# State space matrices and rotation tables made in another layer's stage and kept in DRAM

## The chip, the cores and the metric

The kernel runs on one core of a Trainium2 chip. The metric is the time of one execution on the device in microseconds; the time given is the median of three runs. The core has a matrix engine (TensorE, PE in the profile), a vector engine (VectorE, DVE), an activation engine (ScalarE, ACT), a general engine (GpSimd, POOL) and a queue that issues most of the DMAs (SyncE, SP). Each engine works through its own instructions in the order in which the program holds them.

## What is computed

A first block of two layers and a second block of one layer run over 1024 positions (and 16 learned ones in the first block) of width 1024, in float32. Each layer of the first block mixes the positions in three ways, gates and joins the results (`mix`) and adds an output product:

```python
for l in range(DEPTH):                       # 2
    u = rms_norm(h, norm_w[l]) @ w_in[l]
    ...                                      # three mixers, each times silu of a gate
    h = h + mix @ w_out[l]
```

The second block has four branches of width 256; the change is about the first, a diagonal state space with 16 groups of 64 complex states, whose matrices depend on the weights alone:

```python
mag = jnp.exp(lam_re * dt); ang = lam_im * dt
lb_re = mag * jnp.cos(ang); lb_im = mag * jnp.sin(ang)
den = jnp.square(lam_re) + jnp.square(lam_im); nr = lb_re - 1.0
f_re = (nr * lam_re + lb_im * lam_im) / den
f_im = (lb_im * lam_re - nr * lam_im) / den
bb_re = f_re[..., None] * b_re - f_im[..., None] * b_im
bb_im = f_re[..., None] * b_im + f_im[..., None] * b_re
bu_re, bu_im = ...                           # inputs times bb
_, _, x_re, x_im = lax.associative_scan(combine, (a_re, a_im, bu_re, bu_im), axis=1)
y = einsum(x_re, c_re) - einsum(x_im, c_im) + d * ug
y = jax.nn.gelu(y.reshape(bsz, s, BRANCH_WIDTH))
y = y * jax.nn.sigmoid(y @ glu_w + glu_b)
```

The other branches are two attentions and a recurrent mixer; then come gates (32 products of 1024 by 1024 positions, `sigmoid(gates)`), a merge, and a feed-forward part.

## The kernel before, in words

Activations lie with 128 channels on the partitions and positions along the free axis, so a matrix of width 1024 is eight tiles. A float32 product is three passes: values and weights are split into a high and a low part (`hh`, `hl`; `wih`, `wil`), and high by high, low by high and high by low are added in one PSUM bank (L159 to L161). ACT makes the high part of a weight, GpSimd the low one (L153). Tiles come from shared pools: 29 slots, 11 temporaries (`temp`), 6 weight tiles, 2 side tiles; a tile that is asked for waits until the oldest of its pool is free.

*The output products of a layer* (`first_half`): for each of eight row tiles f, `proj` (L163) multiplies the eight tiles of `mx` by the weight `wo`, in three chunks of 348 positions. VectorE adds the residual to each chunk (`hn`, L788), and once all three are done the tile goes to DRAM (`spill`) and is normed in part (`hh` on ACT, `hl` and the sum of squares `sq` on VectorE). `proj` takes a function `along`, which it calls in the middle and at the end of each chunk; here nothing is given.

*The state space's stage* (class `S5`). The positions are cut by four: four neighbours are stacked on the partitions, so 256 steps remain for the scan. `into` shuffles the products of the first weight, 32 channels at a time, into `su`, in turn on ACT and VectorE. `small` works out the powers of the transition from 8-column tiles (62 tiny instructions of VectorE). `matrices` multiplies these into the input matrices `b` (VectorE) and the output matrices `d` (GpSimd), `turned` transposes `b` on TensorE (`s5t`) into `e`, `tables` builds two pairs of rotation tables of 256 steps by doubling (`s5cos`, `s5sin`; the first on VectorE, the second on GpSimd), and `within` makes the matrix `k` of what a step does to itself and its three neighbours (`s5k`). Then `run` walks four blocks of states through `two`, a generator of five steps: input products `bu` on TensorE; a rotation by the tables, with two of its adds on GpSimd (`sw`); four scans on VectorE; the rotation back (`sx`), one of its adds on GpSimd; the output products `sy`. Two blocks are under way at a time, one step behind each other. `gate` applies gelu and the sigmoid gate.

*The gate products* are a filler: `c.feed(us)` puts gate matmuls (`fg`, with weights `fw` split by ACT and VectorE) worth so many microseconds into TensorE's program where it is called, from one list of 512 triples of products that starts in the recurrent stage and whose remainder is worked off after the attentions. In the state space's stage it is called between the steps of `two`.

The order of each engine's instructions is the scheduler's: it follows the order in which the code asks for them, but puts an instruction ahead where its inputs are there early.

Of the kernel before, what the change touches and what calls it, by code (L numbers as in the profile page):

```python
# [12 lines left out]
F32 = mybir.dt.float32  # L13
# [643 lines left out]
def first_half(c, a, vec):  # L657
# [4 lines left out]
    for l in range(2):  # L662
# [799 lines left out]
class S5:  # L1462
# [8 lines left out]
    T = 4  # L1471
    N = 256

    def __init__(self, c, a, project, consts, dcol):
        self.c, self.a, self.dcol = c, a, dcol
        self.u = [c.slot("su") for _ in range(2)]
        self.k = c.slot("s5k")
        c.nc.gpsimd.memset(self.k[:, :1024], 0.0)
        self.small()
        project(0, self.into(self.u[0]))  # L1480
        self.matrices()
        project(1, self.into(self.u[1]))
        self.turned()
        self.tables()
        c.feed(4)
        self.within()
# [18 lines left out]
    def small(self):  # L1505

        c, nc, a = self.c, self.c.nc, self.a
        v = nc.vector
        TT = v.tensor_tensor
        par = c.cp.tile([P, 24], F32, name="s5par", tag="s5par", bufs=1)  # L1510
        nc.sync.dma_start(out=par, in_=a["s5_par"])
        self.bc = bc = c.temp("s5bc")
        nc.sync.dma_start(out=bc[:, :1024], in_=a["s5_bc"])
        lre, lim, ldt = (par[:, 8 * i : 8 * i + 8] for i in range(3))
        sm = c.cp.tile([P, 176], F32, name="s5sm", tag="s5sm", bufs=1)
        w = iter(sm[:, 8 * i : 8 * i + 8] for i in range(22))
        dt, mag, ang, k, si, co = (next(w) for _ in range(6))
        nc.scalar.activation(dt, ldt, AF.Exp)
        TT(mag, lre, dt, ALU.mult)
        nc.scalar.activation(mag, mag, AF.Exp)  # L1520
        TT(ang, lim, dt, ALU.mult)

        v.tensor_scalar(k, ang, 1.0 / (2 * math.pi), 12582912.0, ALU.mult, ALU.add)
        v.tensor_scalar(k, k, -12582912.0, None, ALU.add)
        for part in TURN:
            v.scalar_tensor_tensor(ang, k, -part, ang, ALU.mult, ALU.add)
        v.tensor_scalar(ang, ang, PI_BELOW, -PI_BELOW, ALU.min, ALU.max)
        nc.scalar.activation(si, ang, AF.Sin)
        nc.scalar.activation(co, ang, AF.Sin, scale=0.5)
        TT(co, co, co, ALU.mult)  # L1530
        v.tensor_scalar(co, co, -2.0, 1.0, ALU.mult, ALU.add)
        nr, li, den, t1, fre, fim = (next(w) for _ in range(6))
        TT(nr, mag, co, ALU.mult)
        TT(li, mag, si, ALU.mult)

        pw = c.cp.tile([P, 4 * 32], F32, name="s5pw", tag="s5pw", bufs=1)
        x = [pw[:, 32 * i : 32 * i + 32].rearrange("p (j l) -> p j l", j=8) for i in range(4)]
        self.up, self.down = x[:2], x[2:]
        (ur, ui), (dr, di) = self.up, self.down
        v.tensor_copy(ur[:, :, 0], nr)  # L1540
        v.tensor_copy(ui[:, :, 0], li)
        for l in range(1, 4):
            TT(ur[:, :, l], ur[:, :, l - 1], nr, ALU.mult)
            TT(t1, ui[:, :, l - 1], li, ALU.mult)
            TT(ur[:, :, l], ur[:, :, l], t1, ALU.subtract)
            TT(ui[:, :, l], ur[:, :, l - 1], li, ALU.mult)
            TT(t1, ui[:, :, l - 1], nr, ALU.mult)
            TT(ui[:, :, l], ui[:, :, l], t1, ALU.add)
        v.memset(dr[:, :, 3], 1.0)
        v.memset(di[:, :, 3], 0.0)  # L1550
        for o, i in ((dr, ur), (di, ui)):
            for s in range(3):
                v.tensor_copy(o[:, :, s], i[:, :, 2 - s])

        self.m4, self.c4, self.s4 = (next(w) for _ in range(3))
        TT(self.m4, mag, mag, ALU.mult)
        TT(self.m4, self.m4, self.m4, ALU.mult)
        c2, s2 = (next(w) for _ in range(2))
        for ci, si_, co_, so_ in ((co, si, c2, s2), (c2, s2, self.c4, self.s4)):
            TT(co_, si_, si_, ALU.mult)  # L1560
            v.tensor_scalar(co_, co_, -2.0, 1.0, ALU.mult, ALU.add)
            v.scalar_tensor_tensor(so_, si_, 2.0, ci, ALU.mult, ALU.mult)

        v.tensor_scalar(nr, nr, -1.0, None, ALU.add)
        TT(den, lre, lre, ALU.mult)
        TT(t1, lim, lim, ALU.mult)
        TT(den, den, t1, ALU.add)
        v.reciprocal(den, den)
        TT(fre, nr, lre, ALU.mult)
        TT(t1, li, lim, ALU.mult)  # L1570
        TT(fre, fre, t1, ALU.add)
        TT(fre, fre, den, ALU.mult)
        TT(fim, li, lre, ALU.mult)
        TT(t1, nr, lim, ALU.mult)
        TT(fim, fim, t1, ALU.subtract)
        TT(fim, fim, den, ALU.mult)
        self.fre, self.fim = fre, fim

        self.dq = c.cp.tile([P, 8], F32, name="s5dq", tag="s5dq", bufs=1)
        d2 = self.dq.rearrange("p (t j) -> p t j", t=2)  # L1580
        for s in range(4):
            for j in range(4):
                nc.scalar.copy(d2[32 * s : 32 * s + 32, :, j], self.dcol[32 * j : 32 * j + 32, :])

    def matrices(self):

        c, nc = self.c, self.c.nc
        v, g = nc.vector, nc.gpsimd
        bc = self.bc
        q = lambda x: x.rearrange("p (j h) -> p j h", j=8)  # L1590
        bre, bim, cre, cim = (q(bc[:, 256 * i : 256 * i + 256]) for i in range(4))
        f = lambda x: x.unsqueeze(2).to_broadcast([P, 8, 32])
        bb = c.temp("s5bb")
        o = [q(bb[:, 256 * i : 256 * i + 256]) for i in range(4)]
        TT = v.tensor_tensor
        TT(o[0], bre, f(self.fre), ALU.mult)
        TT(o[2], bim, f(self.fim), ALU.mult)
        TT(o[0], o[0], o[2], ALU.subtract)
        TT(o[1], bim, f(self.fre), ALU.mult)
        TT(o[3], bre, f(self.fim), ALU.mult)  # L1600
        TT(o[1], o[1], o[3], ALU.add)
        every = lambda x: x.unsqueeze(2).to_broadcast([P, 8, 4, 32])
        power = lambda x: x.unsqueeze(3).to_broadcast([P, 8, 4, 32])
        r4 = lambda x: x[:, :1024].rearrange("p (j l h) -> p j l h", j=8, l=4)

        def product(e, re, im, xr, xi, p, sign):

            t = c.temp("s5t")
            e.tensor_tensor(r4(re), every(xr), power(p[0]), ALU.mult)
            e.tensor_tensor(r4(t), every(xi), power(p[1]), ALU.mult)  # L1610
            e.tensor_tensor(re[:, :1024], re[:, :1024], t[:, :1024], ALU.subtract)
            t = c.temp("s5t")
            e.tensor_tensor(r4(im), every(xr), power(p[1]), ALU.mult)
            e.tensor_tensor(r4(t), every(xi), power(p[0]), ALU.mult)
            if sign > 0:
                e.tensor_tensor(im[:, :1024], im[:, :1024], t[:, :1024], ALU.add)
            else:
                v.scalar_tensor_tensor(im[:, :1024], im[:, :1024], -1.0, t[:, :1024], ALU.mult, ALU.subtract)

        self.b = [c.temp("s5b") for _ in range(2)]  # L1620
        product(v, *self.b, o[0], o[1], self.down, 1)
        self.d = [c.slot("s5d") for _ in range(2)]
        product(g, *self.d, cre, cim, self.up, -1)

        self.d0 = c.cp.tile([P, 512], F32, name="s5d0", tag="s5d0", bufs=1)
        nc.scalar.copy(self.d0[:, 0:256], bc[:, 512:768])
        nc.scalar.activation(self.d0[:, 256:512], bc[:, 768:1024], AF.Copy, scale=-1.0)

    def turned(self):

        c, nc = self.c, self.c.nc
        self.e = [c.slot("s5e") for _ in range(2)]
        for r in range(2):
            for h in range(2):
                ps = c.bank("s5t")
                for j in range(4):
                    o = slice((4 * h + j) * P, (4 * h + j + 1) * P)
                    nc.tensor.transpose(ps[:, j * P : (j + 1) * P], self.b[r][:, o], c.ident)
# [768 lines left out]
```

## Time and profile before

| | us |
|---|---|
| median of three runs (3210.05 to 3212.91) | 3212.78 |
| profiled execution, own time | 3217.63 |
| its span, first to last instruction | 3215.8 |
| TensorE busy | 3100.2 (96%) |
| VectorE busy | 1544.1 (48%) |
| ACT busy | 1146.7 (36%) |
| GpSimd busy | 678.5 (21%) |

The mean granted clock of TensorE is 0.983 of full speed (2.4 GHz); the other level that the profile shows is 1.2 GHz, and a window of 10 us with a clock between 0.5 and 1 is a mixture. All durations below come from the one profiled execution, so a sum of them is a difference against 3217.63, not against the median. Busy times of neighbouring matmuls overlap in the records: a matmul starts before the end of the one before it is written down, so a count of matmuls over a stretch in which TensorE never pauses tells what one costs, and not the mean of the single records. The first layer's output products run from about 490 to 580 us, the state space's stage from about 1576 to 1707.

### The profile page before, as it was taken

What the parts mean: (1) busy time and instruction counts of PE and PEld (TensorE: products, weight loads), DVE (VectorE), ACT (ScalarE), POOL (GpSimd) and SP (SyncE); (2) the same over time, 40 slices, a digit from 0 to 9 for tenths busy, and PEclk for the clock granted to TensorE, in tenths of its full rate; (3) what the DMA queues carried; (4) which work ended last, traced back from release to release, by engine and by line L of the source; (5) the groups of instructions that cost most, each with busy time, mean ns of one, the idle gap of its engine ahead of it and who ended that gap; (6) DMA issues with size and microseconds to landing.
All of it is one profiled execution on the core that took longest, in us unless ns stands there. A gap on an engine that the chain in (4) does not pass through costs nothing. (4 is left out here: it accounts for less than half of the span.)

```text
span 3215.8 us, 43114 instructions
## 1 busy us (share of the span) xinstructions
PE 3100.2 (96%) x17540; PEld 2704.1 (84%) x17540; DVE 1544.1 (48%) x2902; ACT 1146.7 (36%) x2171; POOL 678.5 (21%) x401
## 2 busy tenths in 40 slices
PE   8999999999999999999888998899999999999998
PEld 8999999999999878878767787787778888888887
DVE  4536773353666564363594636745572222222134
ACT  4225662222555342232345545512252122122133
POOL 1222001222200420010252000036543222222211
PEclk9999999999999999999989999999999999999999
DMA  3310013221001411112112011354231111111111
GB/s 117 81 65 26 14 45 122 70 87 61 24 14 60 153 34 57 61 49 65 49 38 67 33 34 33 104 180 149 79 108 66 42 48 54 49 42 49 54 50 53
DMA packets 85845, 207.83 MB, mean 65 GB/s; under 512 B 18428, under 2 KB 25596, under 8 KB 85648
## 3 DMA queue, kind: packets, MB, share of 16 engines
q1 hardware_dynamic: 84160, 200.44, 19.1%
q0 software_dynamic: 1488, 4.64, 0.7%
q8 instruction: 138, 2.26, 0.3%
q14 instruction: 59, 0.48, 0.1%
HBM read 170.80 MB, written 34.24 MB: 64 GB/s over the span
## 5 line engine op out<-in xcount | busy, mean ns | idle before, releaser
L159 PE MATMUL pj<-hh,wih 128*128 128x348 f32 x864 | 278.3, 327 | 10.2 <-ACT wih L151 6.6
L160 PE MATMUL pj<-hl,wih 128*128 128x348 f32 x864 | 281.0, 326 | 0.0
L161 PE MATMUL pj<-hh,wil 128*128 128x348 f32 x864 | 279.9, 325 | 0.7 <-POOL wil L153 0.7
L159 PE MATMUL fg<-xx,fw 128*128 128x512 f32 x512 | 217.3, 424 | 0.0
L161 PE MATMUL fg<-xx,fw 128*128 128x512 f32 x512 | 206.0, 403 | 5.6 <-DVE fw L130 5.6
L159 PE MATMUL pj<-gh,m2h 128*128 128x512 f32 (+1 forms) x560 | 211.3, 377 | 0.0
L160 PE MATMUL pj<-gl,m2h 128*128 128x512 f32 (+1 forms) x560 | 209.8, 375 | 0.0
L161 PE MATMUL pj<-gh,m2l 128*128 128x512 f32 (+1 forms) x560 | 209.7, 374 | 0.0
L160 PE MATMUL fg<-xx,fw 128*128 128x512 f32 x512 | 206.4, 403 | 0.0
L161 PE MATMUL pj<-xx,m1l 128*128 128x512 f32 x512 | 201.8, 394 | 0.0
L160 PE MATMUL pj<-xx,m1h 128*128 128x512 f32 x512 | 201.7, 394 | 0.0
L159 PE MATMUL pj<-xx,m1h 128*128 128x512 f32 x512 | 201.5, 394 | 0.0
L2046 DVE TENSOR_TENSOR r<-pj,r 128x512 f32<-128x512 f32 (+1 forms) x104 | 67.5, 650 | 252.3 <-PE pj L161 252.1
L159 PEld LDWEIGHTS pj<-hh,wih 128*128 128x128 f32 x864 | 164.2, 191 | 11.3 <-ACT wih L151 6.6
L160 PEld LDWEIGHTS pj<-hl,wih 128*128 128x128 f32 x864 | 165.2, 191 | 0.7 <-DVE hl L676 0.7
L161 PEld LDWEIGHTS pj<-hh,wil 128*128 128x128 f32 x864 | 164.9, 191 | 1.0 <-POOL wil L153 1.0
L130 DVE TENSOR_TENSOR ptl<-pt,pth 116x348 fp32r<-116x348 f32 (+2 forms) x268 | 150.3, 586 | 21.1 <-ACT pth L129 16.9
L129 ACT CAST pth<-pt 116x348 fp32r<-116x348 f32 (+2 forms) x268 | 129.0, 514 | 86.2 <-PE pt L583 70.7
L2018 DVE TENSOR_TENSOR ge<-pj,ge 128x512 f32<-128x512 f32 x64 | 44.3, 692 | 231.2 <-ACT ge L2017 231.2
L712 DVE TENSOR_TENSOR u<-pj,r 128x348 f32<-128x348 f32 x108 | 54.3, 517 | 209.2 <-PE pj L161 200.3
L153 POOL TENSOR_TENSOR wil<-wi,wih 128x1024 fp32r<-128x1024 f32 x34 | 83.6, 2460 | 317.8 <-PE pj L160 295.0
L153 POOL TENSOR_TENSOR m1l<-m,m1h 128x1024 fp32r<-128x1024 f32 x32 | 77.7, 2427 | 237.9 <-PE pj L160 237.9
(654 smaller groups left out, 8271.8 us busy)
## 6 DMA issues: line engine op xcount, KB each, us to landing
wo<-in_w_out_dram SPq DMA_DIRECT2D x40, 512.0 KB, 3.4
wi<-in_w_in_dram SPq DMA_DIRECT2D x34, 512.0 KB, 3.6
fr<-in_w_in_dram SPq DMA_DIRECT2D x64, 256.0 KB, 2.9
gates<-fg SPq DMA_DIRECT2D x64, 256.0 KB, 2.1
gs<-gates SPq DMA_DIRECT2D x32, 512.0 KB, 4.1
m<-in_mlp_w_dram SPq DMA_DIRECT2D x32, 512.0 KB, 3.4
m<-in_mlp_w_dram SPq DMA_DIRECT2D x32, 320.0 KB, 3.0
w<-in_w_in_dram SPq DMA_DIRECT2D x18, 512.0 KB, 3.4
```

The costliest lines, as they stand in the source:

```text
L129: nc.scalar.copy(hi, src)
L130: nc.vector.tensor_tensor(lo, src, hi.bitcast(F32), ALU.subtract)
L153: eng.tensor_tensor(lo[:, o], raw[:, o], hi[:, o].bitcast(F32), ALU.subtract)
L159: mm(out, a[0], b[0], start=start, stop=False)
L160: mm(out, a[0], b[1], start=False, stop=False)
L161: mm(out, a[1], b[0], start=False, stop=stop)
L712: nc.vector.tensor_tensor(t[:, lo : lo + n], ps, r[:, lo : lo + n], ALU.mult)
L2018: nc.vector.tensor_tensor(q, ps, r, ALU.mult)
L2046: nc.vector.tensor_tensor(t[:, o], ps, t[:, o], ALU.add)
```

## The change

A new class `S5Matrices` has the code of `small`, `matrices`, `turned`, `tables` and `within` as one generator, `steps`, with 51 yields. `first_half` gets it as `aside` and hands it to the output products of its first layer (and of the second, where nothing is left of it): `proj` calls it twice per chunk, so 48 times, and a loop works off the rest. All of it is VectorE's now, the output matrices and the second table too. The nine results, tiles of 128 by 1024, are stored in DRAM by SP (`keep`); the first stage of the second block loads them (`load`, nine loads into slots). The matrix `k` is made from `bb` and `bc` in place of the last column of `b`, with as many matmuls. `two` has its three GpSimd adds on VectorE. `run` starts two blocks, then calls the second half of the input products (`rest`), and then walks both blocks with 2.0 us of gate products after each step (before: 4, twice 3, then 1.2 after each step).

```diff
-            c.proj(w, mx, chunks, evac)
+            c.proj(w, mx, chunks, evac, along=lambda: next(aside, None))
             nc.sync.dma_start(out=spill[f], in_=n_[:, :LP])
             normed_part(n_, f, nxt, LP, h_new)
+        for _ in aside:
+            pass
...
+class S5Matrices:
+    def keep(self, name, t):
+        self.c.nc.sync.dma_start(out=self.kept[name], in_=t[:, :1024])
+
+    def load(self, name):
+        t = self.c.slot("s5" + name)
+        self.c.nc.sync.dma_start(out=t[:, :1024], in_=self.kept[name])
+        return t
+
+    def steps(self):
+        yield from self.small()
+        yield from self.inputs()
+        yield from self.outputs()
+        for h in range(2):
+            yield from self.tables(h)
...
+    def product(self, re, im, xr, xi, p, sign):
...
+        v.tensor_tensor(r4(re), every(xr), power(p[0]), ALU.mult)
+        yield
+        v.tensor_tensor(r4(t), every(xi), power(p[1]), ALU.mult)
+        yield
+        v.tensor_tensor(re[:, T], re[:, T], t[:, T], ALU.subtract)
+        yield
...
-    def __init__(self, c, a, project, consts, dcol):
-        self.c, self.a, self.dcol = c, a, dcol
+    def __init__(self, c, a, project, made):
+        self.c, self.a, self.m4 = c, a, made.m4
+        self.e = [made.load(f"e{r}") for r in range(2)]
         self.u = [c.slot("su") for _ in range(2)]
-        self.k = c.slot("s5k")
-        c.nc.gpsimd.memset(self.k[:, :1024], 0.0)
-        self.small()
+        self.C, self.S = [made.load("cos0")], [made.load("sin0")]
         project(0, self.into(self.u[0]))
-        self.matrices()
-        project(1, self.into(self.u[1]))
-        self.turned()
-        self.tables()
-        c.feed(4)
-        self.within()
+        self.k = made.load("k")
+        self.d = [made.load(f"d{r}") for r in range(2)]
+        self.C.append(made.load("cos1"))
+        self.S.append(made.load("sin1"))
+        self.rest = lambda: project(1, self.into(self.u[1]))
...
-        g.tensor_tensor(re, re, t0, ALU.add)
         v.tensor_tensor(t1, bu[0], S, ALU.mult)
         v.tensor_tensor(im, bu[1], C, ALU.mult)
-        g.tensor_tensor(im, im, t1, ALU.subtract)
+        v.tensor_tensor(re, re, t0, ALU.add)
+        v.tensor_tensor(im, im, t1, ALU.subtract)
...
-        g.tensor_tensor(xr, xr, t0, ALU.subtract)
         v.tensor_tensor(xi, im, C, ALU.mult)
         v.tensor_tensor(t1, re, S, ALU.mult)
+        v.tensor_tensor(xr, xr, t0, ALU.subtract)
...
-        for _ in range(2):
-            next(work[0])
-            self.c.feed(3)
-        on = [work.pop(0)]
+        next(work[0])
+        next(work[1])
+        self.rest()
+        on = work[:2]
+        del work[:2]
         while on or work:
-            if len(on) < 2 and work:
-                on.append(work.pop(0))
             for g in list(on):
                 if next(g, 0) == 0:
                     on.remove(g)
-                self.c.feed(1.2)
+                    if work:
+                        on.append(work.pop(0))
+                self.c.feed(2.0)
```

TensorE's order in the state space's stage, before, at the end of the second half's products (`pj` with `w2h`, `w2l`): the transposes `s5t` follow, then gate products `fg`.

```order
L161 MATMUL pj_14863<-xx_11277,w2l_14818 128x512
L1638 MATMUL s5t_14906<-ident,s5b_14793 128x128 x4
L1638 MATMUL s5t_14912<-ident,s5b_14793 128x128 x4
L1638 MATMUL s5t_14918<-ident,s5b_14794 128x128 x4
L1638 MATMUL s5t_14924<-ident,s5b_14794 128x128 x4
L159 MATMUL fg_15042<-xx_10869,fw_14519 128x512
```

The same engine now, at the end of the first half's products (`pj_15055`): the input products of the first two blocks (`bu_15108` to `bu_15115`, from `su` and the loaded `s5e`), then the second half's products (`pj_15126`).

```order
L161 MATMUL pj_15055<-xx_11669,w2l_15010 128x512
L1763 MATMUL bu_15108<-su_15002,s5e_2297_14998 128x256
L1763 MATMUL bu_15109<-su_15002,s5e_2298_15000 128x256
L1763 MATMUL bu_15108<-su_15002,s5e_2297_14998 128x256
L1763 MATMUL bu_15109<-su_15002,s5e_2298_15000 128x256
L1763 MATMUL bu_15114<-su_15002,s5e_2297_14998 128x256
L1763 MATMUL bu_15115<-su_15002,s5e_2298_15000 128x256
L159 MATMUL pj_15126<-xx_11261,w2h_15121 128x512
```

The transposes and the gate products between the two halves of the stage are gone from this place, and the second half's products now stand behind `bu`.

VectorE's order in the output products, before, for one row tile: three evictions `hn`, then the norm's `hl` and `sq`.

```order
L788 TENSOR_TENSOR hn_5219<-pj_5220,hr_5217 128x348
L788 TENSOR_TENSOR hn_5219<-pj_5246,hr_5217 128x348
L788 TENSOR_TENSOR hn_5219<-pj_5272,hr_5217 128x348
L676 SCALAR_TENSOR_TENSOR hl_5300<-hn_5219,vec,hh_5299 128x1044
L689 TENSOR_TENSOR sq_5114<-sq_5114,sq_5303 128x1044
```

Now, for the row tile during which the input matrices `s5b` are made:

```order
L790 TENSOR_TENSOR hn_5328<-pj_5329,hr_5326 128x348
L1598 TENSOR_TENSOR s5b_5308<-s5b_5308,s5t_5310 128x1024
L1600 TENSOR_TENSOR s5b_5309<-s5bb_5275,s5pw 128x1024
L790 TENSOR_TENSOR hn_5328<-pj_5357,hr_5326 128x348
L1602 TENSOR_TENSOR s5t_5310<-s5bb_5275,s5pw 128x1024
L1605 TENSOR_TENSOR s5b_5309<-s5b_5309,s5t_5310 128x1024
L790 TENSOR_TENSOR hn_5328<-pj_5385,hr_5326 128x348
L678 SCALAR_TENSOR_TENSOR hl_5421<-hn_5328,vec,hh_5420 128x1044
L691 TENSOR_TENSOR sq_5175<-sq_5175,sq_5424 128x1044
```

Between two evictions there are now two instructions of 1024 columns.

ACT's order at the start of the program, before, from the fourth x tile's square on: the cast of a weight, then the next x tiles.

```order
L685 ACTIVATE sq_148<-h_142 128x1044
L151 CAST wih_378<-wi_377 128x1024
L675 ACTIVATE hh_153<-h_151,vec 128x1044
L685 ACTIVATE sq_157<-h_151 128x1044
L675 ACTIVATE hh_162<-h_160,vec 128x1044
```

Now, the same place, with the parts of `small` (`s5sm`, `s5par`) in it:

```order
L687 ACTIVATE sq_158<-h_152 128x1044
L151 CAST wih_388<-wi_387 128x1024
L1512 ACTIVATE s5sm<-s5par 128x8
L1583 COPY s5sm<-s5par 32x2 x16
L1514 ACTIVATE s5sm<-s5sm 128x8
L1522 ACT_TABLE_LOAD
L1522 ACTIVATE s5sm<-s5sm 128x8
L677 ACTIVATE hh_163<-h_161,vec 128x1044
L687 ACTIVATE sq_167<-h_161 128x1044
L1523 ACTIVATE s5sm<-s5sm 128x8
L677 ACTIVATE hh_172<-h_170,vec 128x1044
```

The tiny instructions of `small` have moved from the state space's stage to the very start, on ACT as shown and on VectorE between the same x tiles. On SP the two stores of `e` and the first of `d` stand in one group ahead of the load of the weight `wo` two tiles on, and the second store of `d` ahead of the next one.

## Rows read from the trace of the kernel before

**Rows 1.** windows of one core, state space's stage; columns: span, busy us per engine (instructions), clock, DMA.
```profile
1576.40:1707.20 130.80, 101.15 (x615) 81.12 (x613) 106.20 (x232) 58.91 (x122) 64.35 (x71) 0.90 0.14 46
...
1610.00:1620.00 10.00, 9.07 (x40) 7.42 (x41) 9.01 (x26) 5.71 (x14) 9.53 (x21) 0.67 0.00 1
...
1630.00:1640.00 10.00, 4.36 (x20) 3.24 (x18) 9.62 (x30) 1.38 (x3) 0.95 (x1) 0.86 0.00 0
1640.00:1650.00 10.00, 9.61 (x33) 7.42 (x33) 9.69 (x15) 1.19 (x2) 2.55 (x2) 0.80 0.32 107
1650.00:1660.00 10.00, 6.53 (x22) 5.34 (x23) 10.00 (x15) 1.10 (x3) 5.20 (x3) 0.83 0.09 27
...
1690.00:1700.00 10.00, 9.71 (x37) 7.94 (x38) 0.78 (x1) 6.31 (x10) 0.23 (x1) 0.83 0.14 46
```

**Rows 2.** what TensorE waits for in that stage; columns: us in all, times, longest.
```profile
PE s5t L1638 <- DVE s5b L1611: 11.6, 1, 11.6
PE sy L1752 <- POOL sx L1742: 8.1, 3, 3.9
PE fg L161 <- DVE fw L130: 5.6, 1, 5.6
```

**Rows 3.** windows, then VectorE's and GpSimd's lines, in the output products.
```profile
490.00:580.00 90.00, 89.32 (x561) 89.02 (x560) 34.24 (x42) 26.53 (x27) 19.32 (x8) 1.00 0.42 143
...
L788 DVE TENSOR_TENSOR hn<-pj,hr 128x348 f32<-128x348 f32 x24 | 12.3, 517 | 43.5 <-PE pj L161 43.5
...
L153 POOL TENSOR_TENSOR wol<-wo,woh 128x1024 fp32r<-128x1024 f32 x6 | 14.5, 2420 | 122.1 <-PE pj L160 122.1
```

**Rows 4.** VectorE's lines in the stage's first half; busy, mean ns | idle before.
```profile
L1499 DVE COPY su<-pj 32x128 f32<-32x128 f32 x32 | 9.2, 288 | 1.6 <-ACT su L1501 0.6
L1659 DVE TENSOR_TENSOR s5tm<-s5cos,s5sin 128x4 f32<-128x4 f32 (+7 forms) x8 | 4.0, 503 | 0.3
...
L1704 DVE TENSOR_TENSOR s5k<-s5k,s5kd 32x512 f32<-32x512 f32 (+3 forms) x8 | 3.9, 487 | 0.2
...
L1658 DVE TENSOR_TENSOR s5sin<-s5sin,s5cos 128x4 f32<-128x4 f32 (+7 forms) x8 | 2.2, 280 | 0.0
...
L1609 DVE TENSOR_TENSOR s5b<-s5bb,s5pw 128x1024 f32<-128x1024 f32 x1 | 1.2, 1224 | 0.0
```

**Rows 5.** VectorE's lines in the stage's second half.
```profile
L1736 DVE TENSOR_TENSOR_SCAN sw<-s5sm,sw 128x256 f32<-128x256 f32 x16 | 14.0, 936 | 0.4 <-POOL sw L1727 0.4
...
L1741 DVE TENSOR_TENSOR st<-sw,s5sin 128x512 f32<-128x512 f32 x4 | 2.7, 680 | 0.0
```

**Rows 6.** TensorE's line of the transposes; window with the k products alone.
```profile
L1638 PE MATMUL s5t<-ident,s5b 128*128 128x128 f32 x16 | 3.9, 426 | 12.3 <-DVE s5b L1611 11.6 <-DVE s5b L1616 0.7
...
1620.00:1630.00 10.00, 4.20 (x224) 3.97 (x221) 1.03 (x2) 0.00 (x0) 1.00 0.01 3
```

**Rows 7.** VectorE's and GpSimd's timelines beside each other; start, duration, instruction.
```profile
1588.43 0.17 DVE L1547 TENSOR_TENSOR s5sm<-s5pw,s5sm 128x8 f32<-128x8 f32 x1
...
1597.85 1.98 DVE L1571 TENSOR_TENSOR s5sm<-s5sm 128x8 f32<-128x8 f32 x1
...
1597.43 2.37 POOL L1611 TENSOR_TENSOR s5d<-s5d,s5t 128x1024 f32<-128x1024 f32 x1
```

**Rows 8.** ACT's lines in the state space's stage.
```profile
L1583 ACT COPY s5dq<-vec 32x2 f32<-32x2 f32 x16 | 3.1, 191 | 0.2
...
L1528 ACT ACT_TABLE_LOAD x1 | 1.3, 1283 | 0.0
```

**Rows 9.** ACT's and VectorE's timelines at the program's start.
```profile
22.85 1.17 ACT L675 ACTIVATE hh<-h,vec 128x1044 fp32r<-128x1044 f32 x1 [2.80 <-DMA h<-in_x_dram]
...
39.34 0.27 ACT L219 ACTIVATE ir<-ms,eps 116x9 f32<-116x9 f32 x1 [5.09 <-PE ms L218]
...
33.95 1.24 DVE L689 TENSOR_TENSOR sq<-sq,sq 128x1044 f32<-128x1044 f32 x1
```

**Rows 10.** the page's DMA issues; columns: count, KB each, us to landing.
```profile
wo<-in_w_out_dram SPq DMA_DIRECT2D x40, 512.0 KB, 3.4
```

More of the change, by code (lines that the diff above doesn't have):

```diff
@@ L654, in attend, with first_half @@
                 pass
-def first_half(c, a, vec):
+def first_half(c, a, vec, aside):
     nc = c.nc
@@ L1503, in into @@
         return put
[L1505 to L1638, printed above, removed]
-                nc.scalar.copy(self.e[r][:, h * 512 : h * 512 + 512], ps)
-    def tables(self):
-        c, nc = self.c, self.c.nc
-        N = self.N
-        self.C, self.S = [], []
-        for h, e in enumerate((nc.vector, nc.gpsimd)):
-            cos, sin, tm = c.slot("s5cos"), c.slot("s5sin"), c.temp("s5tm")
-            C, S, X = (x[:, : 4 * N].rearrange("p (j t) -> p j t", j=4) for x in (cos, sin, tm))
-            e.tensor_copy(C[:, :, 0], self.c4[:, 4 * h : 4 * h + 4])
-            e.tensor_copy(S[:, :, 0], self.s4[:, 4 * h : 4 * h + 4])
-            n = 1
-            while n < N:
-                b = lambda x: x[:, :, n - 1 : n].to_broadcast([P, 4, n])
-                lo, hi, th = slice(0, n), slice(n, 2 * n), slice(0, n)
-                e.tensor_tensor(C[:, :, hi], C[:, :, lo], b(C), ALU.mult)
-                e.tensor_tensor(X[:, :, th], S[:, :, lo], b(S), ALU.mult)
-                e.tensor_tensor(C[:, :, hi], C[:, :, hi], X[:, :, th], ALU.subtract)
-                e.tensor_tensor(S[:, :, hi], S[:, :, lo], b(C), ALU.mult)
-                e.tensor_tensor(X[:, :, th], C[:, :, lo], b(S), ALU.mult)
-                e.tensor_tensor(S[:, :, hi], S[:, :, hi], X[:, :, th], ALU.add)
-                n *= 2
-            self.C.append(cos)
-            self.S.append(sin)
@@ L1708, in two @@
     def two(self, b, y):
         c, nc = self.c, self.c.nc
-        v, g = nc.vector, nc.gpsimd
+        v = nc.vector
         N = self.N
@@ L1837, in gate_filler, with second_half @@
         made.add(tile_of(f))
-def second_half(c, a, hx, old, vec2, out):
+def second_half(c, a, hx, old, vec2, made_s5, out):
     nc = c.nc
@@ L1873, in second_half @@
         with c.phase("s5"):
-            s5 = S5(c, a, project, None, vec2["s5_d"])
+            s5 = S5(c, a, project, made_s5)
             y = [c.slot("ys") for _ in range(2)]
@@ L2384, in tile_network @@
     nc.sync.dma_start(out=vec, in_=a["vec"])
+    s5 = S5Matrices(c, a, c.cp.tile([P, 8], F32, name="s5m4"))
     with c.phase("mixing"):
-        hx, old = first_half(c, a, vec)
-    second_half(c, a, hx, old, load_vec2(c, a["vec2"]), out)
+        hx, old = first_half(c, a, vec, s5.steps())
+    second_half(c, a, hx, old, load_vec2(c, a["vec2"]), s5, out)
 def kernel(**inputs):
```

243 lines of the change are left out of this document (200 added, 43 removed).

## The prediction

> **What bounds the kernel now.** The page's busy shares come first: TensorE is busy for nearly all of the span and the next engine, VectorE, for half of it, so almost everywhere only TensorE's own work counts. The change is about two stretches where that can differ, so I read each by itself. The windows view of the state space's stage, from its first product pj to the first product of the next stage's values (1576.4 to 1707.2), gives 130.80 us with TensorE busy for 101.15: 29.65 us idle, while VectorE is busy for 106.20 [rows 1]. The waits of TensorE there say for whom: 11.6 us once, for the matrix s5b that VectorE makes; 8.1 us in three waits for sx, which GpSimd finishes; 5.6 us for a gate weight's split queued on VectorE behind the tables [rows 2]. The stage is therefore bound by VectorE and the chains through it, not by TensorE. A second loss is hidden in its busy time: the granted clock is 0.67, 0.86, 0.80, 0.83 and 0.83 in five of the 10-us windows, each of which begins, or comes after, an idle stretch [rows 1]. The busy time of each times what is missing of the clock (9.07 x 0.33, 4.36 x 0.14, 9.61 x 0.20, 6.53 x 0.17, 9.71 x 0.17) is 3.0 + 0.6 + 1.9 + 1.1 + 1.7 = 8.3 us.
>
> The stretch that receives the work is the other one: the first layer's output products, 490 to 580. There TensorE is busy for 89.32 of 90 us at clock 1.00, VectorE for 34.24, GpSimd for 19.32 [rows 3]. VectorE's idle time before the 24 evictions hn is 43.5 us, all of it spent waiting for TensorE [rows 3].
>
> **What the change removes from the state space's stage.** Gone from it are the 62 tiny VectorE instructions, twelve product instructions (five were GpSimd's), both tables, the four groups of transposes s5t and the k products s5k. With them goes the 11.6 us wait for s5b and the 5.6 us wait for fw, which stood behind the table on VectorE. What is late next I look for in the new order. TensorE's first bu products stand right behind the first product pj and need its shuffled copies su: 32 on VectorE of 0.288 us [rows 4] and as many on ACT, 8 of each per chunk of 512 columns. Only the last 8 are left when pj ends, of which TensorE covers little, since the bu rows come first: 1 to 2 us. Then the second half's products, 11 us, cover the first two blocks on VectorE, which cost each twelve instructions of 0.680 us, the three adds that come from GpSimd among them, and four scans of 0.936: 8.2 + 3.7 = 11.9 us a block by busy time, and a little less where one starts before the other's record ends, so 22 to 24 for two [rows 5]. Those two blocks, the 16 remaining su copies (4.6 us) and three gate splits of the same width (2 us) stand on VectorE, 30 us in all, before the first sy, and TensorE has ahead of it 11 us of pj and 54 gate products fg. One fg matmul I take at 0.23 us (a matmul of 348 columns is 89.32 / 561 = 0.159 us in the output products [rows 3], times 512/348), so 12.4 us: cover of 23 to 24 from the end of the first product, plus 9 fg before each next sy. What is left uncovered is about 1 us at each of the first sy, one gate split and the third sy, and 1.5 us at each of the two ends that remain as they are (the gelu chain's wait for ygh and the next stage's for fxvl): 6 to 8 us where 29.65 were, I take 7. The clock loss then goes from 8.3 to about 1, since no idle stretch as long as those is left. So: 29.65 - 7 = 22.7, and 7.3 of clock: 30.0 us. The bounds: 22.7 + 7.3 is what goes if VectorE's new chain fits as above; if all the three sy waits and the fw wait stay (8.1 + 5.6) it is about 16 with half the clock, and if nothing at all stays idle 29.65 + 8.3 = 38.
>
> **What it moves without gain.** The s5t groups are 3.9 us of TensorE at the low clock (two at full) and the s5k groups 4.2 us [rows 6], 7 us with the gaps between them. They leave the stage and are spent in the output products, where TensorE has no idle time to put them in: +7 - 7 = 0. The gate products handed out in the stage rise from 172 to 204; 32 x 0.23 = 7.4 us appear in it and go from the pure product stretch at the end: again 0. So the stage by itself should get shorter by 30.0 + 7 - 7.4 = 29.6 us, to about 101.
>
> **What it costs in the output products.** VectorE gets twelve instructions like L1609's 1.224 us (14.7), six of a quarter of that width (2.5), the k additions with their diagonal, two more of 512 columns (3.9 + 1.4) and two tables [rows 4]. A table is six lines of eight instructions each; the line least disturbed took 2.2 us, the most disturbed 4.0 [rows 4], so 13 to 24 us a table; I take 13, since the disturbance is GpSimd's own table, which is gone. Together 14.7 + 2.5 + 5.3 + 26 = 49 us beside the 34.24 that are there: 83 of the 97 us that the stretch will have with the moved matmuls, 105 with the other end. It fits, but not evenly: each step stands in VectorE's queue ahead of an eviction hn, so a group of three 1.22-us instructions delays an eviction by up to 3.7 us. A chunk of TensorE lasts 3.8 us (561 matmuls in 89.32 us, 24 a chunk [rows 3]) and there is more than one bank, so one such delay is hidden; TensorE's s5t and s5k rows, which wait for s5b and s5d, have a margin of about a microsecond each. I book 0.5 us, with bounds 0 and 8.
>
> In this stretch GpSimd makes one wol of 2.42 us per weight [rows 3]. The row beside it in the state space's stage shows what such a neighbour can do: VectorE's instruction on 8 columns at 1597.85 took 1.98 us and ended when GpSimd's of 2.37 us did, and the same kind took 0.17 where GpSimd was idle [rows 7]. So each of the 8 wol may hold VectorE for up to 2.4 us: at most 19 us, and 83 + 19 = 102 of 97, which would put the last evictions 5 us behind TensorE, still less than the 10 us and more that the next stage's first products, which go through the eight tiles in turn, leave them. The term stays 0.5, and this is where its upper bound of 8 comes from.
>
> The Trainium skill's page "SBUF — State Buffer", section "Who interferes with whom", says that a VectorE instruction with two SBUF inputs and a GpSimd instruction that reads SBUF share one read interface, and that the later one is blocked until the earlier is through. This case's row agrees: the instruction of 8 columns that took 1.98 us. By that rule the change puts all its tables beside wol, which speaks against it (up to 19 us of holding), and takes GpSimd's products, table and adds away from beside VectorE in the state space's stage, which speaks for it; by the rule alone the sum would be some 5 us worse than mine in the first stretch if the evictions had no slack.
>
> **What it costs at the start.** The scheduler puts the tiny instructions at the very beginning of the program. ACT gets 16 copies of 0.191 us, four activations as short and one table load of 1.283 [rows 8]: 5.1 us in all, between two x tiles, where it idled 2.80 us for a DMA [rows 9]. VectorE gets 62 instructions, 0.08 to 0.17 us each: 5 to 10 us, where it idles for as long as ACT waits for that x tile. Its last sum of squares would end 4 to 6 us after 35.19; what waits for it is ACT's root at 39.34, which came 5.09 us after ACT's last work because TensorE was busy with other products [rows 9], so the first 3 to 4 us of it are covered. I take +2.0, bounds 0 and 6.
>
> **Sum.** -22.7 - 7.3 + 0.5 + 2.0 = -27.5 us against the profiled execution, 3217.63 us (span 3215.8). The three timed runs have a median of 3212.78, 4.85 lower, and the saving is a difference, so I set it off against that: 3185.3.
>
> **The rivals.** (1) VectorE stays the bound of the state space's stage. The three adds per block that were GpSimd's now stand in VectorE's own chain, in series with the scans. For it: VectorE was busy 106 of 131 us, and the two blocks' first results now come at the same time, late. Against it: some 50 us of its work are gone from the stage. Then the sy waits (8.1) and the fw wait (5.6) remain, and half of the clock's loss: 29.65 - 13.7 - 3 = 13 and 4 of clock, less the 2.5 of costs: -14 to -15, 3198. (2) Everything is covered: no stalls and no clock loss in the stage, nothing lost elsewhere but the start: 38 - 2.5 = -35.5, 3177. (3) The loads of the tables come late. They are nine transfers of 512 KB each on SP's queue, and a slot must be free for each; where e0 and e1 wait for the slots of the stage before, the first bu waits as s5b was waited for. A transfer of that size lands in 3.4 us [rows 10]; four ahead of the first product, 11 to 14 us, must be issued by about its start. If they are not: up to 11.6 us stay and clock with them, -12, 3201; with the costs of the other bounds (8 and 6) on top, within 0.2% of before. (4) The other side: the output products are stalled. The place is SP's queue: the stores of s5e and s5d wait there for VectorE, ahead of the loads of two output weights. A weight is used for 11.5 us, three chunks, and its wol of 2.42 us starts when the weight before it comes into use (what ends wol's wait is TensorE's pass over the older one [rows 3]), so about 9 us are its slack. From 9 us of lateness of VectorE on TensorE waits for each of the last five weights; 20 us of table work at the upper end and 19 of holding by GpSimd make that possible, 7 us a weight: 35 us, and with the clock's fall after each idle stretch more than 35: 3185 + 35 = 3220. Against it: VectorE's idle 43.5 us before the evictions, and that both stores' tiles are made in the first half of the stretch.
>
> **How the numbers follow.** Chances: the forecast 0.64, with its own range 3178 to 3193; rival 1 0.16; rival 2 0.08; rival 3 0.07; rival 4 0.05. A measurement of this kernel tells 0.2% from no change, 6.4 us. The forecast, rivals 1 and 2 and half of rival 3 are faster by more than that: 0.64 + 0.16 + 0.08 + 0.035 = 0.915, from which I take 0.015 for several costs at their bounds at once, so 0.90; that and the other half of rival 3 are within: 0.05; rival 4 is slower: 0.05. For eight in ten the range takes in the forecast, most of rival 1 and most of rival 2: 3174 to 3203.
>
> **What would show it.** In the changed profile: the window from the first product of the state space's stage to the next stage's values near 101 us, TensorE idle in it near 7, clock 0.95 or more throughout; no wait for s5b; waits for sx of under 1.5 us each, now released by VectorE. In 490 to 590: TensorE busy within 1 us of the whole, VectorE 80 to 90 us busy, the waits of TensorE for s5b or s5d under 1 us. At the start: ACT's root 1 to 4 us after 39.34. I am wrong if TensorE waits in the output products for more than 8 us, or for su, sx or e for more than 15 us in all, or if the clock stays under 0.9 there.

## The result and the profile after

The changed kernel takes 3186.11 us, median of four runs (3182.69 to 3187.91), where the kernel before takes 3212.85; the ratio is 0.9913 with a 95% interval of 0.9898 to 0.9927, so 23 to 33 us less. 3185.3 was forecast. Its profiled execution took 3187.91 us with a span of 3186.2, 29.6 less than the span before.

The state space's stage first. The window over the whole of it, in the columns of [rows 1]:

```profile
1587.42:1690.50 103.08, 97.06 (x407) 77.48 (x406) 62.24 (x111) 50.92 (x96) 4.47 (x4) 0.97 0.26 91
...
1680.00:1690.00 10.00, 6.47 (x18) 4.77 (x17) 2.88 (x3) 6.05 (x8) 2.01 (x1) 0.66 0.22 70
```

103.08 us where 130.80 were; TensorE idle for 6.0 where it was 29.65; VectorE busy for 62 where it was 106, GpSimd for 4.5 where it was 64. Only one of its 10-us windows still has a low clock, the last. What TensorE waits for there (columns as in [rows 2]):

```profile
PE pj L159 <- ACT ygh L129: 3.5, 1, 3.5
PE bu L1763 <- issue: 1.3, 1, 1.3
PE v L160 <- POOL fxvl L153: 0.7, 1, 0.7
PE sy L1796 <- DVE sx L1789: 0.5, 1, 0.5
PE fg L161 <- DVE fw L130: 0.4, 1, 0.4
PE bu L1763 <- DVE su L1746: 0.2, 1, 0.2
```

(The line for v falls just behind the window's end.) The 11.6 us for s5b are gone, the 8.1 us for sx are 0.5, the 5.6 us for fw are 0.4. The largest wait left is the one at the end, for the cast of the gelu's result; it was shorter in the kernel before:

```profile
PE pj L159 <- ACT ygh L129: 1.6, 1, 1.6
```

The output products, from the first eviction to 90 us later and from there to the next layer's root (columns as in [rows 3]):

```profile
495.50:585.50 90.00, 90.00 (x767) 89.41 (x765) 74.72 (x159) 25.03 (x28) 18.55 (x9) 1.00 0.48 166
585.50:611.10 25.60, 24.12 (x158) 23.75 (x156) 9.98 (x11) 4.47 (x4) 4.76 (x2) 1.00 0.40 136
```

Two lines of VectorE's timeline in it, and one of GpSimd's:

```profile
509.95 2.99 DVE L1596 TENSOR_TENSOR s5t<-s5bb,s5pw 128x1024 f32<-128x1024 f32 x1
515.66 1.21 DVE L1598 TENSOR_TENSOR s5b<-s5b,s5t 128x1024 f32<-128x1024 f32 x1
```

```profile
509.45 2.40 POOL L153 TENSOR_TENSOR wol<-wo,woh 128x1024 fp32r<-128x1024 f32 x1 [9.06 <-PE pj L160]
```

TensorE is busy without a gap for 90 us, VectorE for 74.72 of them where it was 34.24. One product of VectorE took 2.99 us in place of 1.21, because it began while GpSimd's wol was running: it ended 1.1 us after wol, which is nearly its own length. That happened to one more of them (2.98 us), and to three instructions of the tables, each beside GpSimd's work on a weight (wol or wil):

```profile
561.75 2.66 DVE L1698 TENSOR_TENSOR s5tm<-s5sin 128x256 f32<-128x256 f32 x1
573.29 2.34 DVE L1701 TENSOR_TENSOR s5cos<-s5cos,s5tm 128x4 f32<-128x4 f32 x1
585.65 2.73 DVE L1698 TENSOR_TENSOR s5tm<-s5sin 128x512 f32<-128x512 f32 x1
```

Instructions of these widths take 0.41, 0.17 and 0.68 us elsewhere in the tables, so the five were held for about 10 us in all. TensorE waited for none of them. But it went the other way too: GpSimd's split wil that stood beside the last of the three took 3.16 us in place of 2.40, and TensorE's wait for it, its only one in the stretch, is 1.4 us where it was 0.7:

```profile
584.68 3.16 POOL L153 TENSOR_TENSOR wil<-wi,wih 128x1024 fp32r<-128x1024 f32 x1 [9.07 <-PE pj L160]
```

```profile
PE pj L161 <- POOL wil L153: 1.4, 1, 1.4
```

The start, against [rows 9]: ACT's timeline, VectorE's, and TensorE's waits in the first 100 us.

```profile
20.00 3.23 ACT L1583 COPY s5sm<-s5par 32x2 f32<-32x2 f32 x16
...
23.48 1.28 ACT L1522 ACT_TABLE_LOAD   x1
...
24.89 1.15 ACT L677 ACTIVATE hh<-h,vec 128x1044 fp32r<-128x1044 f32 x1
...
43.77 0.27 ACT L219 ACTIVATE ir<-ms,eps 116x9 f32<-116x9 f32 x1 [9.30 <-PE ms L218]
```

```profile
39.19 1.24 DVE L691 TENSOR_TENSOR sq<-sq,sq 128x1044 f32<-128x1044 f32 x1
```

```profile
PE pj L159 <- ACT hh L677: 4.1, 2, 2.9
PE pj L160 <- DVE hl L678: 3.3, 2, 1.8
```

Before, the first of these two waits was shorter and the second was not there:

```profile
PE pj L159 <- ACT hh L675: 3.0, 1, 3.0
```

ACT reaches the x tile 2.0 us later than before, VectorE's last sum of squares ends 5.2 us later and the root comes 4.4 us later. TensorE waits 3.3 us for hl, for which it did not wait before, and 1.1 us longer for hh; together that is the 4.4.

The whole span by stages. Idle is what TensorE is not busy; the clock's loss is its busy time in 5-us windows, each times what its granted clock lacks of 1.

| stage, ended by | length before, after | idle | clock's loss |
|---|---|---|---|
| start, first root | 39.3, 43.8 | 9.6, 14.2 | 0, 1.3 |
| first layer, first eviction of its output products | 451.5, 451.7 | 3.5, 3.8 | 4.6, 4.5 |
| its output products, next root | 108.4, 115.6 | 0.7, 1.5 | 0, 0 |
| second layer, first eviction of its output products | 437.6, 435.8 | 3.2, 3.6 | 3.0, 0 |
| these, and the recurrent branch | 539.0, 540.6 | 9.2, 9.2 | 5.9, 7.5 |
| state space, first value product v | 131.4, 103.0 | 29.7, 6.0 | 7.7, 2.6 |
| attentions and left gate products, last fg | 507.4, 494.6 | 29.6, 30.0 | 5.4, 0 |
| the rest | 1001.1, 1001.1 | 30.1, 31.0 | 12.7, 12.0 |

In sum +4.4 + 0.2 + 7.2 - 1.8 + 1.6 - 28.4 - 12.8 = -29.6.

### The profile page after: what moved, and what is told of

Read it like the earlier page. It is cut to its first block, busy times and chain, and to the rows that moved or that the text cites. A ratio compares the mean times of both kernels' runs of the same rounds, so it can differ in the third digit from the quotient of the medians.

```text
span 3186.2 us, 43136 instructions
## 1 busy us (share of the span) xinstructions
PE 3086.9 (97%) x17540; PEld 2690.9 (84%) x17540; DVE 1557.8 (49%) x2969; ACT 1142.5 (36%) x2169; POOL 618.9 (19%) x334
## 5 line engine op out<-in xcount | busy, mean ns | idle before, releaser
L543 DVE TENSOR_REDUCE mx<-sc 116x1 f32<-116x348 f32 (+3 forms) x204 | 104.9, 514 | 40.2 <-PE sc L542 37.6
```

Source lines behind the costliest of these rows:

```text
L543: nc.vector.tensor_reduce(mx[:n, x : x + 1], o, AX.X, ALU.max)
```

## The experiments

All are edits of the changed kernel, timed in five rounds unless said. The theory: the stage was held up by VectorE and by chains through it and GpSimd, and what is moved away costs next to nothing where it goes. The rivals: it is the rewrite of `two` and `run`, not the move; there is no room where the work goes; the clock is chance.

**The adds on GpSimd again.**

```diff
-        v.tensor_tensor(re, re, t0, ALU.add)
-        v.tensor_tensor(im, im, t1, ALU.subtract)
+        nc.gpsimd.tensor_tensor(re, re, t0, ALU.add)
+        nc.gpsimd.tensor_tensor(im, im, t1, ALU.subtract)
...
-        v.tensor_tensor(xr, xr, t0, ALU.subtract)
+        nc.gpsimd.tensor_tensor(xr, xr, t0, ALU.subtract)
```

> The changed kernel with the three adds per block of the state space given back to GpSimd; all else as changed. Theory A (the gain is VectorE's relief from tables and matrices, and two blocks in step cover each other): VectorE works on the other block while GpSimd adds, so the waits for sx grow by 0 to 4 us in all, span 3186 to 3190. Rival B (the adds themselves were what TensorE waited for, 8.1 us in three waits for sx before): those waits come back with part of the clock's loss, span 3194 to 3198.

3194.22 us, ratio 0.9933 (0.9920 to 0.9947), span 3194.8; the stage takes 109.9 us with 11.8 idle. By the time rival B is right: the three adds are worth 7 us of the stage (109.9 against 103.0). By the waits each theory has a part: of 5.7 us more of idle time the wait for sx makes 3.3 (0.5 became 3.8, which theory A allowed), and 3.2 are for the gate weights' splits fw, which neither named. TensorE's waits in it, then GpSimd's three lines and two of VectorE's:

```profile
PE sy L1796 <- POOL sx L1788: 3.8, 1, 3.8
PE fg L161 <- DVE fw L130: 1.8, 1, 1.8
PE fg L159 <- ACT fw L129: 1.8, 1, 1.8
```

```profile
L1788 POOL TENSOR_TENSOR sx<-sx,st 128x512 f32<-128x512 f32 x4 | 11.4, 2851 | 15.9 <-issue 9.3 <-DVE st L1785 6.6
L1774 POOL TENSOR_TENSOR sw<-sw,st 128x512 f32<-128x512 f32 x4 | 6.3, 1568 | 3.6 <-DVE sw L1772 3.6
L1773 POOL TENSOR_TENSOR sw<-sw,st 128x512 f32<-128x512 f32 x4 | 5.2, 1288 | 29.7 <-DVE sw L1770 29.7
```

```profile
L1780 DVE TENSOR_TENSOR_SCAN sw<-s5m,sw 128x256 f32<-128x256 f32 x16 | 13.3, 888 | 0.0
...
L1786 DVE TENSOR_TENSOR sx<-sw,s5cos 128x512 f32<-128x512 f32 x4 | 4.6, 1141 | 0.1
```

The mean of 2.85 us hides one very long add. The other three of that line took 1.26 to 1.30 us, and the eight for sw 1.27 to 1.69; this one took 7.55, and TensorE's wait for sx ended with it:

```profile
1665.45 7.55 POOL L1788 TENSOR_TENSOR sx<-sx,st 128x512 f32<-128x512 f32 x1 [4.80 <-issue]
```

```profile
1673.05 1.13 PE L1796 MATMUL sy<-sx,s5d 128*128 128x255 f32 x4 [3.76 <-POOL sx L1788]
```

VectorE ran ten instructions with two SBUF inputs back to back from 1665.24 to 1671.87; the add ended 1.13 us after the last of them, nearly its own length. In the kernel before the adds for sx took 2.2 to 3.9 us, and most of those for sw 1.3 to 1.7. VectorE takes 0.69 us for such an add, and it is not relieved by giving them away: the scans take 0.888 us on average, before 0.936 [rows 5], and with the adds on VectorE 0.693, by the changed kernel's lines:

```profile
L1780 DVE TENSOR_TENSOR_SCAN sw<-s5m,sw 128x256 f32<-128x256 f32 x16 | 10.3, 693 | 0.1
...
L1788 DVE TENSOR_TENSOR sx<-sx,st 128x512 f32<-128x512 f32 x4 | 2.8, 689 | 0.1
```

16 scans at 0.195 us and four L1786 at 0.45 are 4.9 us of VectorE lost to GpSimd's adds; twelve adds of 0.69 are 8.3. VectorE's busy time in the stage is 60.0 with the adds away and 62.2 with them. The Trainium skill's "SBUF — State Buffer", section "Who interferes with whom", says that a VectorE instruction with two SBUF inputs contends with a GpSimd instruction that reads SBUF. The trace agrees: the add of 7.55 us and the longer scans.

**The old order of the blocks**, with the loaded matrices.

```diff
-        self.rest = lambda: project(1, self.into(self.u[1]))
+        project(1, self.into(self.u[1]))
+        c.feed(4)
...
-        next(work[0])
-        next(work[1])
-        self.rest()
+        for _ in range(2):
+            next(work[0])
+            self.c.feed(3)
...
-                self.c.feed(2.0)
+                self.c.feed(1.2)
```

> The changed kernel with the order of before around the blocks: both halves of the input products first, then gate products worth 4, 3 and 3 us and 1.2 after each step, one block a step behind the other; tables and matrices still made early and loaded. Theory A1 (relief alone carries the gain): no table is in the way, TensorE waits under 10 us in the stage, span 3186 to 3190. Theory A2 (the new order's cover is needed too: a block's chain on VectorE takes some 12 us and 1.2 us of gate products a step do not cover it): waits for sx and su of 12 to 20 us and clock loss of 3 to 5, span 3198 to 3208.

3193.77 us, ratio 0.9933 (0.9921 to 0.9946), span 3190.0. In the stage A1 holds: 95.9 us with 6.5 idle and 175 gate products; 29 more of them would make it 102.6. So the new order itself gives nothing there, and A2 is wrong. But all five runs (3189.42 to 3195.97) lie above all eight of the changed kernel in this document (3181.43 to 3188.49), so the old order does cost some 8 us outside the stage. In the profiled execution the difference lies in the attentions: 508.2 us with a clock's loss of 7.3, against 494.6 with none; 6.7 us of it are the 29 gate products. The part on the prediction comes back to it.

**The small parameters late.**

```diff
-        par = c.cp.tile([P, 26], F32, name="s5par")
+        par = c.temp("s5par")
```

> The changed kernel with the tile of the state space's small parameters taken from the pool of temporaries, so that the 62 tiny VectorE instructions, 16 ACT copies and the table load stand at the beginning of the output products and not at the program's start. Theory A (they cost 4.4 us at the start, in TensorE's waits for hh and hl): ACT's first root is back at about 39.4 us, the output products lose 0 to 2 us by a fuller VectorE, span 3181 to 3184. Rival C (VectorE has no room left there, 76 of 90 us are busy): the transposes and k products wait for s5b and s5d by 3 to 6 us, span 3185 to 3189.

3180.44 us, ratio 0.9894 (0.9880 to 0.9908), span 3176.5: theory A, with a span 4.5 us under its range. The median is 5.7 us under the changed kernel's (3.4 under that of its repeat below), though the intervals of the two ratios overlap; 4.7 of the span's 9.7 us lie at the start; another 4.7 are less clock's loss in the recurrent branch, a loss that moved by 2.2 between two executions of the changed kernel as well. The start and the output products say it more sharply: ACT's root at 39.03, no wait for hl, and the output products with VectorE 4.3 us fuller not a microsecond longer. ACT's timeline and the window of the output products of this run, then that window of the changed kernel:

```profile
39.03 0.27 ACT L219 ACTIVATE ir<-ms,eps 116x9 f32<-116x9 f32 x1 [5.11 <-PE ms L218]
```

```profile
489.26:604.54 115.28, 114.13 (x922) 113.16 (x920) 89.03 (x213) 29.59 (x33) 23.03 (x10) 1.00 0.46 160
```

```profile
495.50:611.10 115.60, 114.12 (x922) 113.16 (x920) 84.69 (x169) 29.50 (x32) 23.30 (x10) 1.00 0.46 159
```

**All of it in the state space's stage**, on VectorE, without DRAM.

```diff
-            c.proj(w, mx, chunks, evac, along=lambda: next(aside, None))
+            c.proj(w, mx, chunks, evac)
...
-        for _ in aside:
-            pass
...
+        for _ in made.steps():
+            pass
```

> The changed code, but all matrices and tables are made at the beginning of the state space's stage, on VectorE, in slots, without DRAM; new order of the blocks and adds on VectorE as changed. Theory A (moving the work away is the gain): VectorE has its 62 us and some 55 more in the stage, and the first bu, which stand ahead of the second half's products, wait for e: the stage takes 125 to 145 us, span 3205 to 3225. Rival B (the rewrite for VectorE and the new order are the gain, GpSimd's neighbourhood was the cost): 105 to 112 us, span 3186 to 3193.

3223.57 us, ratio 1.0031 (1.0020 to 1.0042), span 3220.2: theory A. Without the move the rewritten code, in this order, makes the kernel slower than before; the same code beside the output products takes 37 us less. The matrices are made ahead of the stage's first product pj here: from that product on the stage takes 126.6 us, and from the last products of the recurrent branch on some 154, with 46 idle, where the changed kernel takes 103. TensorE's two largest waits:

```profile
PE s5t L1631 <- DVE s5b L1594: 20.7, 1, 20.7
PE bu L1761 <- DVE su L1744: 18.4, 1, 18.4
```

The kernel before had this work between the two halves of the products and gave part of it to GpSimd, so this run does not tell what a better order within the stage would give. The adds are worth 7 us of the stage's 28 and the order nothing, which leaves some 21 for the move, by difference; no run has the move without the rewrite.

**Less of the gate products as cover.** `feed(2.0)` becomes `feed(1.2)`.

> The changed kernel with gate products worth 1.2 us after each step of the blocks in place of 2.0 (33 in place of 54 ahead of the first sy, 39 in place of 63 ahead of the third). Theory A (VectorE's chain of two blocks is just covered by 11 us of the second half's products and the gate products): 21 x 0.23 = 5 us less cover at the first sy and 24 x 0.23 = 5.5 at the third become waits for sx, 8 to 11 us of idle more in the stage and 2 to 4 of clock: span 3196 to 3202. Rival B (the cover was ample): under 3 us more idle. In either case some 80 gate products more are left for the stages behind; theory D (the clock in the attentions' stage fell in before and in the run with the old order, both with 545 or more gate products left, and not with 516) expects a granted clock of 0.97 to 0.98 there, 5 to 7 us; rival E (the clock's falls are chance of one execution) expects no relation.

3200.79 us (3192.78 to 3202.11), ratio 0.9953 (0.9941 to 0.9966), span 3191.0. Theory A, at half the size: idle 10.4 us in the stage, 4.4 more, and with 128 gate products where there were 204 it takes 92.3 us, which with the other 76 (17.6 us) would be 109.9, 6.9 more. The profiled execution was the fastest of the five, so it shows only 4.8 of the 14.7 us by which the median lies above the changed kernel's; the other four had a mean granted clock of 0.986 to 0.988, this one 0.989. Theory D's 5 to 7 us of clock in the attentions came to 3.9. Its waits for sx:

```profile
PE sy L1796 <- DVE sx L1788: 4.7, 2, 2.7
```

**The wait for ygh covered**, on top of the small parameters late.

```diff
         yx = [c.split_new("yg", y[s], 1024, c.temp) for s in range(2)]
+        c.feed(5)
```

> As the run with the small parameters late, and besides gate products worth 5 us asked for between the gelu and the gate's products at the end of the state space's stage. Theory A (the wait for ygh, 3.5 us, lacks cover only): the wait goes and the low clock behind it (1 to 2 us) too, span 5 us under that run, 3171 to 3174, median near 3175. Rival F (the wait is ACT's queue: the sigmoid of the gate products and their two table loads stand between the gelu and the cast of ygh, and more gate products bring more of them): the wait stays at 2 to 4 us, span as that run.

The wait shrinks to 0.6 us, the low clock at the end is gone, and the stage takes 102.85 us with 225 gate products; the 21 more are 4.9 us, so 4.7 us are saved as theory A has it. The wait, and the window of the stage:

```profile
PE pj L160 <- DVE ygl L130: 0.6, 1, 0.6
```

```profile
1586.37:1689.22 102.85, 99.77 (x427) 79.36 (x426) 63.21 (x112) 51.53 (x97) 4.51 (x4) 1.00 0.29 95
```

The time does not show it: 3179.15 us, ratio 0.9888 (0.9873 to 0.9904), against 0.9894 for the run without it; near 3175 was expected. In the profiled execution, the slowest of the four (span 3181.1), the recurrent branch lost 9.0 us to the clock, in the run without it 2.9. It is the lowest median of all, not distinguishable from the one before it.

**More work beside the output products.** Eight of twelve product instructions are issued twice (three rounds), in the lines of this form:

```diff
         v.tensor_tensor(r4(re), every(xr), power(p[0]), ALU.mult)
+        v.tensor_tensor(r4(re), every(xr), power(p[0]), ALU.mult)
```

> The changed kernel with eight of the twelve product instructions issued twice (the same result written again), 9.8 us more of VectorE in the first half of the output products. Theory A (the stretch is filled to about 76 of 90 us and the order is in line: the k products s5k start 0.2 us after s5d is done): TensorE waits for s5d by 3 to 7 us, the stretch from the first eviction to the next layer's root grows from 115.6 to 119 to 123 us. Rival G (what VectorE is late is hidden by banks and loads ahead): under 1 us more.

3190.22 us, ratio 0.9928 (0.9914 to 0.9941). Theory A: the stretch takes 120.8 us in place of 115.6, and TensorE waits where it was expected to, for s5d a little less than expected. So the room is used up; 9.8 us more of VectorE at that place cost 5.2, of which 3.1 are idle time and 1.4 clock. TensorE's two new waits:

```profile
PE s5k L1666 <- DVE s5d L1611: 2.5, 1, 2.5
PE s5t L1639 <- DVE s5b L1609: 0.9, 1, 0.9
```

**The changed kernel again** (three rounds).

> The changed kernel once more, unchanged, for a second profile. Theory D (the falls of the clock belong to the order of instructions): stage by stage the idle times within 0.5 us and the clock's losses within 1 us of the first profile, none in the attentions' stage. Rival E (the falls are chance of one execution): idle times as before, clock losses that differ by 2 to 6 us in single stages.

3183.87 us, ratio 0.9909 (0.9895 to 0.9922), span 3182.9. Idle times agree within 0.5 us in most stages (start and attentions 1.2 less, rest 1.3 less), but the clock's loss does not: start 0 after 1.3, first layer 3.0 after 4.5, recurrent branch 5.3 after 7.5, state space 1.4 after 2.6, second layer 1.4 after 0, attentions 1.7 after 0. So a single stage's loss moves by 1 to 2 us between executions of one program: closer to rival E, at a smaller size than it said.

## Why the prediction was right

*The main term* was right: 22.7 us of idle time and 7.3 of clock were to go from the state space's stage; 23.7 and 5.1 went. The idle time that was to remain (some 7 us) is 6.0, but it is made up otherwise. For su, the first and third sy and a gate split 4 to 5 us were forecast; sx, fw, su and the 1.3 us before the first bu came to 2.4. The wait for ygh was put at 1.5 and took 3.5 (the run with cover behind the gelu brings it to 0.6), and the low clock behind it is most of the 2.6 us of clock's loss that are left where about 1 was forecast. The stage was forecast at about 101 us and took 103.

*That the moved matmuls cost nothing more than themselves* held: the output products grew by 7.2 us for 7 that were moved and 0.5 booked. VectorE was to get 49 us of work there and got 50.6, 84.69 us over the whole stretch, where the kernel before has

```profile
490.86:599.29 108.43, 107.72 (x682) 107.34 (x680) 34.06 (x41) 27.23 (x27) 21.72 (x9) 1.00 0.37 126
```

GpSimd's holding, bounded at 19 us, came to about 10 in five instructions, and TensorE waited for none of the five. What it did wait for is the opposite case, which the forecast did not have: 0.7 us more for a wil that was lengthened beside VectorE's work, close to the 0.5 booked. The run with the doubled products shows that this was close: with 9.8 us more the same stretch lost 5.2.

*The start was mis-sized*: "the first 3 to 4 us of it are covered" was wrong. +2.0 was booked and +4.4 came. I had followed only the sum of squares to the root; but TensorE takes the tiles hl one after the other as they come, so each delay of hl is a wait of its own (3.3 us), and 1.1 us more went to hh. The run with the small parameters late takes this work from the start and shows it: the root is back at 39.03, and the wait for hl is gone.

*The clock in the attentions* was not in the sum. The stage there shrank by 12.8 us, of which 7.4 are the 32 gate products that were moved and 5.4 the clock's loss, which was 5.4 before and 0 after. In the window of the kernel before that holds the largest of these losses, and one of the old-order run:

```profile
1947.20:1957.20 10.00, 8.22 (x48) 7.33 (x46) 10.00 (x19) 5.42 (x13) 0.00 (x0) 0.66 0.26 93
```

```profile
1920.70:1930.70 10.00, 7.72 (x42) 6.98 (x43) 10.00 (x19) 4.71 (x11) 0.00 (x0) 0.66 0.24 81
```

Both stand where VectorE is busy throughout and TensorE waits in several pieces. With 545 to 592 gate products left for these stages the loss was 5.4, 7.3 and 3.9 us (before, old order, less cover), with 495 to 516 it was 0 to 3.2 in seven profiles (0 and 1.7 in the two of the changed kernel). That looks like a relation, but the groups nearly touch and there is one profile for each other program. The whole spans speak for it, though not strongly: the ten runs of the old order and of less cover have a mean granted clock of 0.987, the eight of the changed kernel and its repeat 0.989 (two of the other edits 0.988), and 0.0024 of some 3100 busy us is about 7 us, the size of the old order's loss (an estimate from these means). Where in the span it lies, and why, stays open.

So the close hit owes something to two errors of opposite sign: the start took 2.4 us more, the clock behind the stage gave 5.4 more, both by one profile of each kernel, and the single runs of the changed kernel lie up to 7 us apart.

*Rival 1* had VectorE as the bound because of the three adds: the opposite is shown, the adds on VectorE save 7 us of the stage. *Rival 2* (all covered) did not come: the wait for ygh stays. *Rival 3*: no wait for a loaded tile shows. For the 1.3 us before the first bu the profile names no releaser; the tiles e were asked for at 1560.39 and 1562.12 and landed in about 5 us, more than 30 us earlier, and the wait ends 0.1 us after one of VectorE's copies su, so it is more likely one for su. *Rival 4*: the output products have no stall but the one for wil.

## What to carry to other kernels

Work that depends on weights alone belongs beside the stage in which its engine idles, even at the price of a trip through DRAM: here VectorE's work on them cost nothing to speak of where TensorE never waits for it, and the stage that had waited for it became 28 us shorter, while 7 us of TensorE's own work left it and 7 us of gate products came in. See to where the scheduler really puts it, since a tile that comes from no shared pool let small instructions go to the very start here. And a second engine that took over a step in a serial chain was a loss here: it was nearly twice as slow even undisturbed, it held up the first, and the first could hold it up for as long as it ran on without a pause.

## What the runs showed of the hardware

GpSimd's add of 128 by 512 took 1.26 to 1.30 us where nothing held it, VectorE's own 0.69. One such add took 7.55 us while VectorE ran ten instructions with two SBUF inputs back to back, and ended 1.13 us after the last. It goes the other way too: with GpSimd's adds beside them VectorE's scans took 0.888 us on average and not 0.693, a product of 1.21 us took 2.99 beside GpSimd's split of a weight, and an instruction of 4 columns 2.34 in place of 0.17. The granted clock's loss in one stage differs by 1 to 2 us between executions of the same program, as much as many edits are worth, so stages were compared by idle time and length and not by the span alone.
